# RWKV-7 half of a two-layer trunk: TensorE's projections and a recurrence round's ScalarE work put into written-out orders

## The chip, the cores and the metric

The kernel runs on one core of a Trainium2 chip. The metric is the device time of one execution in microseconds (us); lower is better. Each version's time is the median of several runs.

## The reference, cut to what matters

The reference is one inference step of a two-layer trunk on 1104 tokens: a prompt of 1024 tokens behind 16 learned meta tokens, and 8 sampled sequences of 8 tokens each. Layer 0 is a gated DeltaNet layer, which the change does not touch. Layer 1 is RWKV-7 time mixing, of which this much matters here:

```python
xs = xn[None] + xx[None] * mu[:, None, None, :]            # six mixes with the token before
rkvz = jnp.einsum('sbtd,sde->sbte', xs[:4], w_rkvz)        # r, k, v, z: four 1024 x 1024 projections
...
def step(S, inp):
    r_t, k_t, v_t, d_t, kk_t, b_t = inp
    S = (S * d_t[:, :, None, :]
         + jnp.einsum('bhvk,bhk->bhv', S, -kk_t)[..., None] * b_t[:, :, None, :]
         + v_t[..., None] * k_t[:, :, None, :])
    return S, jnp.einsum('bhvk,bhk->bhv', S, r_t)
...
y = (y - mean) * lax.rsqrt(var + GN_EPS) * lnx_w.reshape(H, N) + lnx_b.reshape(H, N)   # per head
y = y + jnp.sum(r_h * k_h * r_k, -1, keepdims=True) * v_h                              # bonus
y = y.reshape(B, T, D) * jax.nn.silu(z)
return y @ w_o, S, xn[:, -1]
```

There are 16 heads of 64. The data is float32.

## The kernel before, in words

**Numbers.** A product of two float32 matrices is made as three matmuls: each factor is split into a high part (a copy by ScalarE, line 86, such as `whi` of a weight tile `wraw`) and the rest (a subtraction on GpSimd, or sometimes VectorE, line 90, such as `wlo`), and high x high, high x low and low x high are summed. A weight tile has 8 blocks of 128 rows, so a projection tile of 128 outputs by up to 384 tokens is 24 matmuls. Tokens come in three segments: 384, 384 and 336.

**The stages of layer 1**, by the time at which they stand in the profile:

- about 1360 to 1475: the decay and rate terms and the key projection (`keys_decay_rate`).
- about 1475 to 1860: the projections r, v and z (`project`; z only for two segments, the third is left to the recurrence). Each starts with `mix`: for 8 blocks of 128 channels and each segment, ScalarE scales the tokens, VectorE adds the scaled tokens before them (tile `mixs`, line 1071), ScalarE takes the high part and VectorE or GpSimd the low one (tiles `xa`, `xc`, `xh`, `xl`). The tiles of a projection's input are reused by the next one. Beside the projections the *systems* are set up (`rwkv_inverse`): the tokens are cut into chunks of 64, six chunks of one pair of heads and one segment are an *item*, and there are 8 pairs x 3 segments = 24 items in five batches. For each item VectorE, ScalarE and GpSimd prepare `skk` and `sal`, TensorE makes 24 small matmuls `fL` (shown as x12 pairs in an order) and two `frss`, and VectorE copies the latter out (`rkc`). For each batch VectorE then inverts blocks by substitution (`invtmp`, `invT`, lines 444 and 446), and a *merge* for each item joins two 32 x 32 inverses into a 64 x 64 one: matmuls `mY`, a VectorE scaling `invY`, matmuls `mU` (`inverse_merge`).
- about 1860 to 2421: the recurrence (`wave`). It runs in rounds, tau = -3 to 53; an item takes six rounds, one for each chunk, a new item starts every second round, and so up to three items of different pairs are in a round. A round is a chain: *solve and scores* on TensorE from the state (`rA<-rS,AR`), `X` on ScalarE (line 62), the *inner* matmuls (`rA<-X,rTT`), `UV` on ScalarE, then the new state and the outputs from `UV` (`rA<-UV,BT` and `rA<-UV,G`), the state update `rS` on VectorE (line 1470), which needs `pre`, the decayed old state, from ScalarE, and the outputs `y` (line 1481). One PSUM tile `rA` of each item holds all of these products. The next round's solve needs `rS`.

**What fills a round.** Between the steps of the chain stand pieces of other work: the preparation of the next item (`rwkv_front`: loads `fldk`, `flda` and others, ScalarE's `fkk`, `fDp`, `fiD`, `k`, `prh`, GpSimd's and VectorE's products, TensorE's `fG`, `fBT`, `fVT`, `fbonus`, and the copies `BT` and `UV` out of PSUM), GroupNorm and the gate of finished items (`rwkv_finish`, whose product `lz` is split into `yh` and `yl` for the output projection), and *jobs* handed out by `fill` at steps that a table of start and end rounds sets: first the gates of the third segment (matmuls `zz`, six to a step), then output projections (`zo` and `do`), each of which starts by splitting two weight tiles on ScalarE and GpSimd.

**What sets the order.** A scheduler simulates the program's time line and puts each engine's instructions in order from that; `high_priority` moves an instruction ahead in its choice. In a block under `manual_schedule` for TensorE, TensorE's instructions stay in the order in which the code emits them. Before the change, the recurrence is under it (so TensorE's order there is the code's, and the other engines' is the scheduler's), and the projections are not: there the scheduler orders all engines. Every engine works through its own list in order and waits at an instruction whose inputs are not ready.

## Time and profile before

| | us |
|---|---|
| median of 3 runs (lowest 2412.68, highest 2417.64) | 2412.91 |
| the profiled execution | 2422.7 |
| its span | 2421.0 |
| granted TensorE clock over the span | 0.967 of full speed |
| TensorE busy | 2213.4 |
| VectorE busy | 1620.5 |
| ScalarE busy | 1279.8 |
| GpSimd busy | 1049.8 |

The profile names TensorE's matmuls PE and its weight loads PEld, VectorE DVE, ScalarE ACT and GpSimd POOL. A row names the engine, the line of the code, the operation and the tiles: `PE L80 rA<-UV,G` is a matmul on line 80 into `rA` from `UV` and `G`. Most matmuls of the recurrence and of the projections are recorded on lines 76 and 80, which are helpers, so they are told apart by their tiles. In a list of waits, "A <- B: 24.0, 47, 2.2" says that A waited for B 24.0 us in all, 47 times, 2.2 us at most. In a time line a bracket at a row's end says how long the engine was idle before that row and for what. Durations of matmuls include their way through the array, so that successive ones overlap.

### The profile page before, as it was taken

To read this page: it belongs to the slowest core of one execution; us is meant where nothing else is said; L and a number is where in the kernel's file an instruction comes from. 1 tells how busy PE (TensorE), PEld (TensorE's weight loads), DVE (VectorE), ACT (ScalarE), POOL (GpSimd) and SP (SyncE) were. 2 spreads that over 40 slices of the span, in tenths; PEclk is the share of its full clock that TensorE was granted. 3 is DMA by queue.
4 is the path that set the end of the run, shared out by engine and by line. 5 is a ranking of instruction groups with operands and counts; after the bars stand their busy time and mean duration, and the time that the engine had idled before them with its cause. 6 is when DMAs were issued, how large, how long until landed. Compare 5 with 4: busy or idle time off the path is not lost. (4 is left out here: it accounts for less than half of the span.)

```text
span 2421.0 us, 54809 instructions
## 1 busy us (share of the span) xinstructions
PE 2213.4 (91%) x19737; PEld 2003.7 (83%) x19737; DVE 1620.5 (67%) x4201; ACT 1279.8 (53%) x3665; POOL 1049.8 (43%) x1446
## 2 busy tenths in 40 slices
PE   6989999999999999999989998988998888888896
PEld 5888989888898989888989898877787676777775
DVE  6868676776868596863347616588894567667654
ACT  5445555555646565565334647474453555666552
POOL 3435343334434353433314424453354555666643
PEclk9999999999999999999999999999998999999998
DMA  3323333323232333353351344666645435555543
GB/s 110 104 74 101 86 109 86 91 76 99 82 108 61 100 96 89 94 160 114 108 137 61 97 172 153 169 160 172 167 122 173 124 107 149 158 163 156 157 131 117
DMA packets 470924, 290.05 MB, mean 120 GB/s; under 512 B 188506, under 2 KB 456027, under 8 KB 470651
## 3 DMA queue, kind: packets, MB, share of 16 engines
q1 hardware_dynamic: 470650, 286.53, 42.0%
q8 instruction: 156, 2.56, 0.5%
q14 instruction: 118, 0.96, 0.1%
HBM read 200.53 MB, written 85.89 MB: 118 GB/s over the span
## 5 line engine op out<-in xcount | busy, mean ns | idle before, releaser
L90 POOL TENSOR_TENSOR wlo<-wraw,whi 128x512 fp32r<-128x512 f32 (+2 forms) x252 | 331.8, 1319 | 379.9 <-ACT whi L86 361.6
L76 PE MATMUL d<-xc,whi 128*128 128x384 f32 (+2 forms) x910 | 258.3, 341 | 4.5 <-POOL xc L90 2.5
L86 ACT CAST whi<-wraw 128x512 fp32r<-128x512 f32 (+2 forms) x252 | 152.0, 605 | 145.4 <-PE dq L76 50.7
L411 DVE SCALAR_TENSOR_TENSOR cvy<-raw,cw,cvy 128x408 f32<-128x408 f32 (+2 forms) x288 | 179.0, 634 | 16.3 <-ACT cvy L62 14.5
L76 PEld LDWEIGHTS d<-xc,whi 128*128 128x128 f32 (+1 forms) x910 | 167.5, 191 | 10.7 <-issue 3.4
L444 DVE TENSOR_TENSOR invtmp<-invA,invT 72x31 f32<-72x31 f32 (+31 forms) x403 | 165.2, 410 | 14.1 <-DMA invA<-ltd 5.3
L446 DVE TENSOR_TENSOR invT<-invT,invtmp 72x31 f32<-72x31 f32 (+31 forms) x403 | 165.7, 411 | 6.6
L76 PE MATMUL dz<-xc,whi 128*128 128x384 f32 (+1 forms) x480 | 148.9, 341 | 0.0
L76 PE MATMUL dv<-xc,whi 128*128 128x384 f32 (+1 forms) x480 | 146.8, 335 | 0.0
L76 PE MATMUL d<-xc,wlo 128*128 128x384 f32 (+2 forms) x428 | 142.3, 341 | 1.4 <-POOL wlo L90 1.4
L76 PE MATMUL d<-xa,whi 128*128 128x384 f32 (+3 forms) x450 | 139.8, 345 | 3.5 <-DVE xa L90 1.7
L860 POOL TENSOR_SCALAR Sb<-Sb,eglb 128x128 f32<-128x128 f32 x128 | 80.1, 643 | 90.4 <-DMA Sb<-in_state_gdn 46.8
L76 PE MATMUL dv<-xa,whi 128*128 128x384 f32 (+1 forms) x288 | 100.0, 347 | 0.1
L76 PE MATMUL dz<-xa,whi 128*128 128x384 f32 (+1 forms) x288 | 100.1, 348 | 0.0
L76 PEld LDWEIGHTS d<-xa,whi 128*128 128x128 f32 (+1 forms) x450 | 83.1, 190 | 11.5 <-issue 4.5
L76 PEld LDWEIGHTS dz<-xc,whi 128*128 128x128 f32 x480 | 89.4, 192 | 0.8
L76 PEld LDWEIGHTS dv<-xc,whi 128*128 128x128 f32 x480 | 88.6, 188 | 0.5 <-issue 0.4
L80 PE MATMUL rA<-UV,G 128*64 128x64 f32 x1152 | 63.6, 240 | 26.0 <-DVE rS L1470 24.0
L76 PE MATMUL d<-xa,wlo 128*128 128x384 f32 (+3 forms) x252 | 85.5, 339 | 0.0
L62 ACT ACTIVATE o<-rA,gcol 128x128 f32<-128x128 f32 x128 | 46.6, 372 | 73.6 <-DVE S L771 73.3
L76 PE MATMUL d<-xh,wlo 128*128 128x384 f32 (+1 forms) x256 | 84.1, 344 | 1.5 <-POOL wlo L90 1.5
L76 PE MATMUL d<-xh,whi 128*128 128x384 f32 (+1 forms) x256 | 84.2, 344 | 0.7 <-ACT whi L86 0.4
(509 smaller groups left out, 7194.7 us busy)
## 6 DMA issues: line engine op xcount, KB each, us to landing
wraw<-in_gdn_w_in SPq DMA_DIRECT2D x96, 256.0 KB
wraw<-in_rwkv_w_rkvz SPq DMA_DIRECT2D x80, 256.0 KB
Sb<-in_state_gdn SPq DMA_DIRECT2D x64, 256.0 KB
wraw<-in_rwkv_w_o SPq DMA_DIRECT2D x40, 256.0 KB
E<-drow SPq DMA_DIRECT2D x24, 384.0 KB
attn<-drow SPq DMA_DIRECT2D x24, 384.0 KB
wraw<-in_gdn_w_out SPq DMA_DIRECT2D x36, 256.0 KB
out_s_gdn<-Sb SPq DMA_DIRECT2D x32, 256.0 KB
```

Of the source, the lines that this page charges most:

```text
L62: return self.nc.scalar.activation(out, in_, func, bias=bias, scale=scale, **kw)
L76: self.nc.tensor.matmul(out, lhsT, rhs, start=start, stop=stop)
L80: self.nc.tensor.matmul(out, lhsT, rhs, start=start, stop=True, skip_group_check=True)
L86: nc.scalar.copy(hi, x)
L90: e.tensor_tensor(lo, x, hi.bitcast(F32), op=ALU.subtract)
L411: nc.vector.scalar_tensor_tensor(y[:, 0:wd], raw[:, k:k + wd], cw[k], y[:, 0:wd], op0=ALU.mult, op1=ALU.add)
L444: nc.vector.tensor_tensor(tmp, A[:, j, j + 1:32].unsqueeze(2).broadcast_to([nb, n, m]), Tv[:, j, 0:m].unsqueeze(1).broadcast_to([nb, n, m] ...
L446: nc.vector.tensor_tensor(Tv[:, j + 1:32, 0:m], Tv[:, j + 1:32, 0:m], tmp, op=ALU.subtract)
L860: nc.gpsimd.tensor_scalar(Sb[:, u], Sb[:, u], self.eglb[:, hv, 4 * g + u:4 * g + u + 1], None, op0=ALU.mult)
```

## The change

It has two parts.

**Projections.** A new method `projections` runs r, v and z with TensorE in emission order. A projection tile is now emitted segment by segment, 24 matmuls each, and after every 12 there is a *gap* (r 48, v 48, z 32 of them). In each gap one step of the systems is emitted: an item is three empty steps and then its `fL` and `frss` in one, a batch ends with four empty steps and its inversion. A batch's merges stand from the 28th gap after that on, one a gap, `mY` in one and `mU` in the next. The last tile of k is emitted in the same manner, without systems. Two stretches of TensorE's order where r gives way to v (`d` are the projection's matmuls, `fL` an item's, `mY` a merge's, `fbpp` a transposition for a batch's scales). Before, with the last rows of r's tile `d_20109` and the first of `d_20809`:

```order
L76 MATMUL d_20109<-xh_2813_15540,wlo_20050 128x336
L76 MATMUL mY_18871<-T1n_18730,L_3313_18731 32x32
L76 MATMUL d_20109<-xl_2814_15541,whi_20049 128x336
L76 MATMUL d_20109<-xh_2815_15542,whi_20049 128x336
L76 MATMUL d_20109<-xh_2815_15542,wlo_20050 128x336
L76 MATMUL mY_18871<-T1n_18730,L_3313_18731 32x32 x11
L73 MATMUL fbpp_19534<-ident_74,invR_19532 128x30
L76 MATMUL d_20109<-xl_2816_15543,whi_20049 128x336
L76 MATMUL fL_20159<-sal_20154,skk_20139 64x64 x12
L76 MATMUL d_20809<-xc_114,whi_20799 128x384
```

After, with the last row of r's tile `d_19895` and the first of v's tile `d_20128`:

```order
L76 MATMUL d_19895<-xl_2816_15543,whi_19794 128x336
L76 MATMUL mY_19920<-T1n_18865,L_3332_18866 32x32 x12
L76 MATMUL fL_19936<-sal_19875,skk_19860 64x64 x12
L76 MATMUL frss_19937<-sgl_19873,hmask_84 2x384
L76 MATMUL d_20128<-xc_114,whi_20118 128x384
L76 MATMUL d_20128<-xc_114,wlo_20119 128x384
L76 MATMUL d_20128<-xc_114,whi_20118 128x384 x2
L76 MATMUL d_20128<-xc_114,wlo_20119 128x384
L76 MATMUL d_20128<-xc_114,whi_20118 128x384
```

Before, single matmuls of a merge stand between single matmuls of a tile, and a tile may begin before another ends; now a tile's segment runs through, and a merge's `mY`, an item's `fL` and its `frss` stand whole in the gap between two.

**Recurrence.** The state and the outputs of an item are emitted together, and then its `rS` and `y`. TensorE's order at the end of a round of three items, before (state products from `BT` for all items, then output products from `G`):

```order
L80 MATMUL rA_29327<-UV_4127_23281,BT_28194 64x64 x2
L80 MATMUL rA_29333<-UV_4128_23282,BT_28504 64x64 x2
L80 MATMUL rA_29340<-UV_4129_23283,BT_28858 64x64 x2
L80 MATMUL rA_29327<-UV_4127_23281,G_28193 64x64 x2
L80 MATMUL rA_29333<-UV_4128_23282,G_28503 64x64 x2
L80 MATMUL rA_29340<-UV_4129_23283,G_28857 64x64 x2
```

After:

```order
L80 MATMUL rA_29249<-UV_4126_23283,BT_27951 64x64 x2
L80 MATMUL rA_29249<-UV_4126_23283,G_27950 64x64 x2
L80 MATMUL rA_29255<-UV_4127_23284,BT_28249 64x64 x2
L80 MATMUL rA_29255<-UV_4127_23284,G_28248 64x64 x2
L80 MATMUL rA_29261<-UV_4128_23285,BT_28563 64x64 x2
L80 MATMUL rA_29261<-UV_4128_23285,G_28562 64x64 x2
```

A round's output products now follow each item's state products at once.

`pre` moves from the end of the solve to behind the inner matmuls (`step_old`), and all of ScalarE's work that the code emits behind the inner matmuls of a round (`issue_after`) is tied behind the last `UV` of that round. The pieces stand in another order: `front` for the next item is emitted at the end of an even round, the gates begin two rounds earlier with an extra step of `fill` in the rounds before tau = 0, `rwkv_finish` has one step more, and a new output projection's weight splits come with the `fill` behind the inner matmuls. ScalarE's order where the second kind of job, an output projection, begins, before (`whi` is the first of its two weight tiles, `X` and `UV` belong to the second round before the one in which its matmuls `zo` start):

```order
L86 CAST whi_28101<-wraw_28099 128x512
L1396 COPY BT_27312<-fBT_27707 128x384
L62 ACTIVATE X_27759<-rA_27758,rk_10_97 128x64
L62 ACTIVATE X_27765<-rA_27764,rk_10_97 128x64
L86 CAST yh_27754<-lz_27418 128x384
L62 ACTIVATE k_5144_27885<-flda_27866,omka_23270,pcol_384 128x384
L62 ACTIVATE X_27772<-rA_27771,rk_10_97 128x64
L62 ACTIVATE UV_4126_23280<-rA_27758 64x128
L62 ACTIVATE UV_4127_23281<-rA_27764 64x128
L62 ACTIVATE UV_4128_23282<-rA_27771 64x128
L62 ACTIVATE fiD_28169<-fldcs_28156 128x384
L86 CAST prh_27894<-pr_27892 128x384
```

After, the rows behind the three `UV` of the round whose matmuls `zo` follow its inner matmuls and read these `whi`:

```order
L62 ACTIVATE pre_28144<-rS_4123_23280,DC_27036 128x64
L62 ACTIVATE pre_28146<-rS_4124_23281,DC_27334 128x64
L62 ACTIVATE pre_28148<-rS_4125_23282,DC_27632 128x64
L86 CAST yh_28150<-lz_27759 128x384
L86 CAST whi_28156<-wraw_28154 128x512
L86 CAST whi_28164<-wraw_28162 128x512
L62 ACTIVATE fkk_28221<-fldk_28213,pcol_384 128x384
L62 ACTIVATE fDp_28223<-fldcs_28211 128x384
L62 ACTIVATE fiD_28224<-fldcs_28211 128x384
L62 ACTIVATE k_5209_28234<-flda_28215,omka_23273,pcol_384 128x384
L86 CAST prh_28243<-pr_28241 128x384
L1501 COPY y_27519<-rA_28097 128x64
```

Before, this split stands two rounds ahead of its use and in front of a round's `X`, and `X`, `yh`, `k` and `X` alternate; now the splits stand behind `UV`, `pre` and `yh`, and `y`, the copies of the round's outputs, stand behind the next item's `fkk`, `fDp`, `fiD`, `k` and `prh`.

Third, GroupNorm's normalisation, two GpSimd operations on 128 x 384 with broadcast operands (lines 1500 and 1501), becomes six operations on 128 x 64 with a scalar for each partition.

```diff
...
+        yield
         pU = self.ps("m", 2, "U")
...
-    def project(self, m, k, x, dst, apart=False):
+    def project(self, m, k, x, dst, gap=None):
         nc, t = self.nc, self.t
-        w = self.load_w(self.i["rwkv_w_rkvz"][0, m][:, 128 * k:128 * k + 128])
-        ps = (self.dense(w, 128, *x, s, bufs=4) for s in range(2 if m == 3 else 3)) if apart else self.dense3(w, 128, *x)
-        for (c0, n), p in zip(SEGS, ps):
+        his, los = w = self.load_w(self.i["rwkv_w_rkvz"][0, m][:, 128 * k:128 * k + 128])
+        ps = zip(SEGS, self.dense3(w, 128, *x)) if gap is None else ((c, self.ps("d", 4)) for c in SEGS[0:2 if m == 3 else 3])
+        for (c0, n), p in ps:
+            if gap is not None:
+                c = 0
+                for q in range(8):
+                    wh, wl = his[q // 4][:, q % 4], los[q // 4][:, q % 4]
+                    a, b = x[0][q][:, c0:c0 + n], x[1][q][:, c0:c0 + n]
+                    for l, r in ((wh, a), (wl, a), (wh, b)):
+                        self.mm(p[:, 0:n], l, r, start=c == 0, stop=c == 23)
+                        c += 1
+                    if q % 4 == 3:
+                        gap()
...
             nc.vector.tensor_tensor(kk, kk, iD, op=ALU.mult)
+            for _ in range(3):
+                yield
             gp = self.ps("f", 2, "L")
...
+        for _ in range(4):
+            yield
         rk2 = self.rk2[:, 30 * b:30 * b + nth]
         blk = self.block_scale(ssd, rk2, pool)
         TT = [t(pool, [128, 6, 64], "sTT", 3) for _ in items]
         T1n, L21 = t(pool, [128, 30, 32], "T1n", 1), t(pool, [128, 30, 32], "L21", 1)
         self.inverse_blocks(f"r{b}", ltd, blk, pool, TT, T1n[:, 0:nth], L21[:, 0:nth], nth)
-        for q, n in enumerate(items):
-            self.inverse_merge(L21, TT[q], T1n, rk2[:, 6 * q:6 * q + 6], pool, 6 * q, 6)
-            nc.sync.dma_start(self.ttd[n], TT[q].rearrange("p c k -> p (c k)"))
+        def merge(q):
+            m = self.inverse_merge(L21, TT[q], T1n, rk2[:, 6 * q:6 * q + 6], pool, 6 * q, 6)
+            next(m)
+            yield
+            next(m, None)
+            nc.sync.dma_start(self.ttd[items[q]], TT[q].rearrange("p c k -> p (c k)"))
+        merges.extend(merge(q) for q in range(len(items)))
...
+    def step_old(self, P, ci):
+        if 6 * P.s + ci > 1:
+            P.pre = self.t(self.ap, [128, 64], "pre", 3)
+            self.act(P.pre, self.S[P.p], AF.Identity, scale=P.DC[:, ci:ci + 1])
...
+        pA, G, BT, UV, S, DC = P.pA, P.G, P.BT, P.UV, self.S[P.p], P.DC
         hs = [slice(0, 64), slice(64, 128)]
+        if c > 0:
+            for h in (0, 1):
+                self.mmx(pA[hs[h], 384:448], BT[:, ci, hs[h]], UV[:, ci, h, :])
         for h in (0, 1):
+            self.mmx(pA[hs[h], 256:320], G[:, ci, h, 64:128], UV[:, ci, h, :])
+        if c > 0:
+            with self.tc.high_priority():
+                if c == 1:
+                    nc.vector.tensor_scalar(S, pA[:, 384:448], DC[:, ci:ci + 1], None, op0=ALU.mult)
+                else:
+                    nc.vector.scalar_tensor_tensor(S, pA[:, 384:448], DC[:, ci:ci + 1], P.pre, op0=ALU.mult, op1=ALU.add)
...
-        b6 = lambda x: x.unsqueeze(2).broadcast_to([128, 6, 64])
-        nc.gpsimd.tensor_tensor(y6, y6, b6(mv[:, :, 0]), op=ALU.subtract)
-        nc.gpsimd.tensor_tensor(y6, y6, b6(rs), op=ALU.mult)
+        for q in range(6):
+            nc.gpsimd.tensor_scalar(y6[:, q], y6[:, q], mv[:, q, 0:1], rs[:, q:q + 1], op0=ALU.subtract, op1=ALU.mult)
...
         nc.vector.scalar_tensor_tensor(zg[:, 0:n], t1[:, 0:n], self.lnb[:, p:p + 1], zg[:, 0:n], op0=ALU.add, op1=ALU.mult)
+        yield
         yh, yl = t(self.fin, [128, 384], "yh", 7, F32R), t(self.fin, [128, 384], "yl", 7, F32R)
         self.split(zg[:, 0:n], yh[:, 0:n], yl[:, 0:n])
...
+    def projections(self, xa, xb, ip):
+        slots = {0: (0, 1, 2, 3, 4, 5, 9, 10), 2: (6, 7, 8, 0, 1, 2, 9, 10), 3: range(3, 11)}
+        now, wait, under, merges = [0], [], [], []
+        def systems():
+            for b in range(5):
+                yield from self.rwkv_inverse(b, ip, merges)
+                wait.extend((now[0] + 28 + n, m) for n, m in enumerate(merges))
+                merges.clear()
+        sy = systems()
+        def gap():
+            now[0] += 1
+            for m in under:
+                next(m, None)
+            under.clear()
+            while wait and wait[0][0] <= now[0]:
+                m = wait.pop(0)[1]
+                next(m)
+                under.append(m)
+            next(sy, None)
+        for m in (0, 2, 3):
+            x = self.mix(m, xb, slots[m], SEGS[0:2] if m == 3 else SEGS)
+            for k in range(8):
+                self.project(m, k, x, {0: self.rd, 2: self.vd, 3: self.zd}[m], gap)
+                if (m, k) == (3, 0):
+                    zin = self.gate_inputs(xa, xb)
+        while wait or under:
+            gap()
+        return zin
...
-        jobs = [(gates, 33, -2.5, 14), (lambda: out(0, 0, 4, Z), 17, 14, 22), (lambda: out(0, 4, 8, DD), 17, 22, 30),
+        jobs = [(gates, 33, -4.5, 14), (lambda: out(0, 0, 4, Z), 17, 14, 22), (lambda: out(0, 4, 8, DD), 17, 22, 30),
...
+        def front(tau):
+            if tau % 2 and (tau + 3) // 2 < 24:
                 s, p = divmod((tau + 3) // 2, 8)
                 P[8 * s + p] = self.rwkv_front(p, s)
+        front(-3)
+        for tau in range(-3, 55):
             m = (tau + 2) // 2
             parts = P[m].parts[3 * (tau % 2):3 * (tau % 2) + 3] if 0 <= m < 24 else [[], [], []]
             items = [(P[n], tau - 2 * n) for n in range(max(0, (tau - 4) // 2), min(24, tau // 2 + 1)) if 0 <= tau - 2 * n < 6]
+            each = lambda *fs: [f(*x) for f in fs for x in items]
+            ins = each(self.step_solve, self.step_scores)
+            if tau < 0:
+                fill(tau + 0.3)
+            for f in parts[0]:
+                f()
+            ins = each(self.step_inner)
+            with self.tc.issue_after(ins[-1]) if ins else ExitStack():
+                each(self.step_old)
+                if tau % 2 == 0 and 0 <= (tau - 8) // 2 < 24:
+                    next(P[(tau - 8) // 2].done, None)
+                fill(tau + 0.5)
+                for f in parts[1]:
+                    f()
+                for Q, ci in items:
+                    if ci == 1 and Q.s == 0:
+                        late.append(self.rwkv_sample_write(Q.p, Q, Q.BT, Q.UV, Q.DC))
+                late = [x for x in late if not next(x, True)]
+                each(self.step_state)
+                fill(tau + 1)
+                for f in parts[2]:
                     f()
                 late = [x for x in late if not next(x, True)]
+                for Q, ci in items:
+                    if ci == 5:
+                        Q.done = self.rwkv_finish(Q.p, Q.s, Q)
+                        next(Q.done)
+                if tau % 2 and 0 <= (tau - 7) // 2 < 24:
+                    next(P[(tau - 7) // 2].done)
+                front(tau + 1)
         fill(99)
```

More of the change, by code (lines that the diff above doesn't have):

```diff
@@ L1748, in layer1 @@
         self.rwkv_masks(ip, True)
[L1749 to L1758 removed]
+        with tc.manual_schedule(engines={mybir.EngineType.PE}):
+            zin = self.projections(xa, xb, ip)
         ctx.close()
@@ L1845, in wave @@
                     f()
                 late = [x for x in late if not next(x, True)]
-                if g == 0:
-                    for Q, ci in items:
-                        if ci == 1 and Q.s == 0:
-                            late.append(self.rwkv_sample_write(Q.p, Q, Q.BT, Q.UV, Q.DC))
-                            next(late[-1])
-            for Q, ci in items:
-                if ci == 5:
-                    Q.done = self.rwkv_finish(Q.p, Q.s, Q)
-                    next(Q.done)
-            if (tau - 7) % 2 == 0 and 0 <= (tau - 7) // 2 < 24:
-                next(P[(tau - 7) // 2].done, None)
```

47 lines of the change are left out of this document (3 added, 44 removed).

## The prediction, made before the changed kernel was run

> **What bounds the kernel now.** I read the page first, then the busy times by stage, then what TensorE (PE) waits for in each stage, and last the time line of two rounds.
>
> ```profile
> span 2421.0 us, 54809 instructions
> PE 2213.4 (91%) x19737; PEld 2003.7 (83%) x19737; DVE 1620.5 (67%) x4201; ACT 1279.8 (53%) x3665; POOL 1049.8 (43%) x1446
> PE 17%; DVE 6%; DMA 3%; issue 2%; ACT 1%; POOL 1%; SPq 0%; DVEq 0%; POOLq 0%; ACTq 0%
> ```
>
> TensorE is busy for 91% of the span and leads the chain, so what can be won without taking matmuls away is its idle time and its slow clock. The change touches the time from 1475 us on. By stage (us, busy time and count of PE, PEld, DVE, ACT, POOL; then granted clock, DMA share, GB/s):
>
> ```profile
> 1475.00:1860.00 385.00, 350.99 (x3297) 309.15 (x3295) 278.38 (x589) 198.09 (x427) 169.54 (x255) 0.95 0.61 159
> 1860.00:1900.00 40.00, 30.03 (x254) 25.65 (x254) 23.91 (x44) 16.36 (x36) 24.45 (x35) 0.83 0.55 164
> 1900.00:2380.00 480.00, 420.90 (x5587) 358.46 (x5583) 321.23 (x903) 268.58 (x853) 271.00 (x306) 0.97 0.49 145
> 2380.00:2421.00 41.00, 23.25 (x139) 20.09 (x139) 17.08 (x43) 10.18 (x28) 14.01 (x20) 0.83 0.22 70
> ```
>
> In the projections TensorE idles 385 - 351 = 34 us and loses about 5% of 385 = 19 us to the clock: 53 us. In the recurrence it idles 10 us at the start, 59 us in the steady part and 18 us at the end; the clock takes 3% of 480 = 14 us and 17% of 40 = 7 us. The waits of TensorE in the recurrence (total us, times, longest):
>
> ```profile
> PE rA L80 <- DVE rS L1470: 24.0, 47, 2.2
> PE rA L80 <- ACT X L62: 20.1, 19, 1.9
> PE rA L80 <- DVE X L1440: 5.8, 5, 4.0
> ...
> PE rA L80 <- ACT y L1481: 3.9, 6, 1.5
> ```
>
> **The rS wait goes: -24 us.** At the end of a round stand:
>
> ```profile
> 2145.59 0.78 ACT L62 ACTIVATE UV<-rA 64x128 f32<-64x128 f32 x3
> ...
> 2147.60 0.57 PE L80 MATMUL rA<-UV,BT 128*64 128x64 f32 x12
> 2148.18 0.66 DVE L1470 SCALAR_TENSOR_TENSOR rS<-rA,DC,pre 128x64 f32<-128x64 f32 x3
> ...
> 2148.51 0.72 PE L80 MATMUL rA<-UV,G 128*64 128x64 f32 x12 [0.34 <-DVE rS L1470]
> ...
> 2150.74 0.68 PE L80 MATMUL rA<-rS,AR 64*64 64x64 f32 x15
> ```
>
> The output products into `rA` start only when VectorE has read the state out of the same `rA`, 47 times for 0.5 us. With each item's output products emitted right behind its state products, nothing that VectorE reads lies between them; `rS` follows both, and 2.2 us of filler (2148.51 to 2150.74) still hide it from the next solve. I take the whole row; the bound below is half of it, if `rS`, now later by an item's products, meets the solve.
>
> **The X wait goes: -18 of 20.1 us.** In every second round ScalarE (ACT) is caught by other work while TensorE needs `X`:
>
> ```profile
> 2162.34 0.51 ACT L86 CAST yh<-lz 128x384 fp32r<-128x384 f32 x1 [1.32 <-DVE lz L1509]
> 2162.76 0.70 ACT L62 ACTIVATE k<-flda,omka,pcol 128x384 f32<-128x384 f32 x1
> 2163.37 0.29 ACT L62 ACTIVATE X<-rA,rk 128x64 f32<-128x64 f32 x1
> 2163.69 0.78 ACT L62 ACTIVATE UV<-rA 64x128 f32<-64x128 f32 x3
> 2163.72 0.45 PE L80 MATMUL rA<-X,rTT 128*64 128x64 f32 x4 [1.55 <-ACT X L62]
> ```
>
> `yh`, which itself waited 1.32 us for VectorE, and `k` stand ahead of the third `X`. In the new order they stand behind `UV`, and the three `X` and three `UV` follow one another. I leave 2 us for rounds in which a `y` or a copy of the round before is late.
>
> **The clock behind short waits: -8 us in the recurrence.** The 4 us behind the wait just shown:
>
> ```profile
> 2164.00:2168.00 4.00, 3.96 (x33) 3.27 (x33) 3.07 (x8) 1.44 (x4) 1.92 (x2) 0.58 0.91 275
> ```
>
> A wait of 1.55 us was followed by a granted clock of 0.58: some 1.7 us lost. With most of the X waits gone I take back 8 of the 14 + 7 us; the rest stays with the other waits. The Trainium skill, page "TensorE: Matmul & The Clock Gate", section "Why this matters for your kernels", says that the clock falls only after TensorE was idle for a whole window, above about 3 us. This row disagrees: 1.55 us were enough. By the page these 8 us, and 7 more below, would not come.
>
> **The start: -4 us.** The first rounds have nothing between solve and inner (the DVE X row, 5.8 us). The change puts 24 `zz` matmuls there, each about 0.18 us at the rate quoted below: 4 us of work done inside waits.
>
> **New waits on ScalarE: +17.5 and +6 us.** Durations on ScalarE and GpSimd (count, busy us, mean ns, idle before):
>
> ```profile
> L62 ACT ACTIVATE pre<-rS,DC 128x64 f32<-128x64 f32 x127 | 39.7, 343 | 19.8 <-DVE rS L1470 19.0 <-DVE rS L1468 0.2
> L86 ACT CAST whi<-wraw 128x512 fp32r<-128x512 f32 x49 | 30.4, 621 | 23.1 <-PE zo L76 9.8 <-PE zz L76 5.8 <-PE do L76 5.7
> L62 ACT ACTIVATE fkk<-fldk,pcol 128x384 f32<-128x384 f32 x20 | 12.3, 616 | 20.9 <-DMA fldk<-kd 20.3 <-POOL BK L1356 0.4
> L62 ACT ACTIVATE fiD<-fldcs 128x384 f32<-128x384 f32 x20 | 10.4, 522 | 18.5 <-DVE BK L1355 18.5
> ...
> L90 POOL TENSOR_TENSOR wlo<-wraw,whi 128x512 fp32r<-128x512 f32 x54 | 71.2, 1319 | 49.7 <-ACT whi L86 49.7
> ...
> L1500 POOL TENSOR_TENSOR y<-y,mv 128x384 f32<-128x384 f32 x24 | 20.0, 833 | 39.8 <-ACT y L1481 24.0 <-DVE mv L1495 13.5 <-DVE bnst L1494 2.0
> ...
> L1342 POOL COPY DC<-fDp 128x6 f32<-128x6 f32 x22 | 6.3, 284 | 23.0 <-DVE rS L1470 22.1 <-ACT fDp L62 0.9
> ```
>
> First, an output projection's first weight tile is now split in the round whose `zo` or `do` needs it, right behind the inner matmuls, where it stood two rounds earlier before. From the inner's end: `UV` 0.8 us, three `pre` 3 x 0.34 = 1.0, `yh` 0.5, `whi` 0.6, then `wlo` on GpSimd 1.3: 4.2 us until the first matmul that reads `wlo`. The filler that stands there, six such matmuls and two of the bonus (8 x 0.18 = 1.4 us), covers in other rounds the `UV` copies; here most of it comes after the wait. 4.2 + about 0.7 of it still to run - 1.4 = 3.5 us a switch, five switches (rounds 14, 22, 30, 38, 46): 17.5 us. Bounds: 0, if an earlier `whi` of the running job leaves the round short enough, to 21 (4.2 each).
>
> Second, `y` now stands behind `pre`, `yh`, `whi`, `fkk`, `fDp`, `fiD` and `k` in even rounds: 1.0 + 0.5 + 0.6 + 0.6 + 0.5 + 0.5 + 0.7 = 4.4 us behind `UV`, and a solve writes the `rA` that `y` reads (the row PE rA <- ACT y shows that wait). In the first time line `UV` ended at 2145.59 + 0.78 = 2146.37, and the solve began at 2150.74, 4.4 us later. The margin is nothing; I put 0.3 us on 20 such rounds, 6 us, from 0 to 25 (rival 2).
>
> **GroupNorm: +1 us.** Two operations of 0.83 us become six of 128x64; each lies between 0.28 us (the 128x6 copy) and 0.83, and I take 0.45, nearer the small one: 2.7 us against 1.7 for an item. GpSimd is busy 271 of 480 us in the steady part and hides it; at the end, where nothing else runs, it costs 1 us.
>
> Recurrence: -24 - 18 - 8 - 4 + 17.5 + 6 + 1 = **-29.5 us**.
>
> **Projections: -14 us.** TensorE waits there:
>
> ```profile
> PE fL L76 <- DVE skk L1299: 11.0, 5, 3.4
> PE mY L76 <- DMA T1n<-r_t: 4.7, 3, 4.1
> ```
>
> The new order gives an item three gaps and a merge 28 before TensorE needs them, so these go. What comes in their place is that TensorE can't pass a matmul whose tile of the mix is late. Pieces of the chain, and VectorE where r gives way to v:
>
> ```profile
> 1803.12 17.39 PE d L76 x98
> ...
> 1724.81 0.84 PE fL L76 x24
> 1725.65 0.74 PE frss L76 x2
> ...
> 1749.93 0.50 PE mU L76 x24
> ```
>
> ```profile
> 1586.35 0.54 DVE L1313 COPY rkc<-frss 2x384 f32<-2x384 f32 x1
> ...
> 1625.57 0.49 DVE L90 TENSOR_TENSOR xl<-mixs,xh 128x336 fp32r<-128x336 f32 x1
> ...
> 1636.28 1.37 DVE L446 TENSOR_TENSOR invT<-invT,invtmp 120x231 f32<-120x231 f32 x1
> ```
>
> ```profile
> 1600.00:1650.00 50.00, 44.58 (x504) 37.05 (x504) 47.78 (x95) 36.35 (x85) 27.01 (x35) 0.92 0.62 169
> ```
>
> VectorE is busy 47.78 of 50 us there with 95 instructions, 0.50 us each. In the new order 83 of them stand between the `rkc` of batch 2's first item and the last low part of v's mix: 83 x 0.50 = 42 us (before, 1586.35 to 1626.06: 40 us from the last item of batch 1). TensorE has from that item's `frss` to v's first tile's need of this part 4 segments of 24 at 17.39 / 98 = 0.177 us, two shorter ones at 336/384 of that, three items of 0.84 + 0.74 = 1.6 and five merges of 1.0 us (`mY` and `mU`, 0.50 each): 17.0 + 7.4 + 4.7 + 5.0 - 0.6 = 33.5 us. So it stalls 42 - 33.5 = 8 us. From k to r, where the mix runs likewise just ahead, I put the same 8; from v to z nothing, since only 14 instructions (7 us) stand there against 18 us of matmuls. Merges and items that find VectorE late: 11 us, as much as the `skk` row. The clock keeps 12 of its 19 us. 8 + 8 + 11 + 12 = 39 against 53 now: **-14 us**. Bounds: -33 (only the transition's 8 and the clock stay) to +40 (rival 3).
>
> **The sum.** -29.5 - 14 = -43.5 us on the profiled 2422.7, so 2379; the same on the median 2412.9 gives **2369 us**. A difference of 0.2%, 4.8 us, is about what a measurement of this kernel tells from none.
>
> **The rivals.**
>
> 1. *More is hidden.* The switches cost nothing and neither r-to-v nor late merges and items stall: -43.5 - 17.5 - 8 - 11 = -80, **2333 us**. For it: VectorE is busy only 278 of 385 us over the stage. Against: 47.78 of 50 in the stretch that counts.
> 2. *The copies of y hold the next solve.* In some 20 even rounds `y` also waits behind `fkk` for its load (20.3 us of waiting for `fldk` in the row above, 1 us a time). 1.2 us more in 20 rounds: +24, **2393 us**.
> 3. *Slower: TensorE in order meets VectorE late.* 24 merges follow `mY` with `mU` one gap of 12 x 0.177 = 2.1 us later, and 24 items need `skk` at a set place; VectorE in between may stand in a substitution step of 1.4 us (the row at 1636.28). If each of the 48 meetings costs 1.1 us, 53 instead of 11, and the clock 12 us more, this is +54 on the sum: -43.5 + 54 = +10, **2423 us**. It decides from about 0.9 us a meeting. For it: before, 5 such waits of up to 3.4 us in spite of free order. Against: VectorE's idle share outside the transitions.
> 4. *Nothing measurable*, as when filler is only used up earlier and the rounds grow elsewhere: **2413 us**.
> 5. *The half clock does not hang on the short waits* and stays: 8 + 7 us do not come, -28.5, **2384 us**. Against: the 0.58 behind 1.55 us. This is also what the page named above would give.
>
> **How the numbers follow.** Forecast 0.45 (own range 2341 to 2395: the switches and the late meetings at nothing, -28, one way; `y` at 1 us a round, +14, and half of the rS row, +12, the other), rival 1 0.13, rival 2 0.17, rival 3 0.14, rival 4 0.07, rival 5 0.04. The range 2332 to 2414 leaves out half of rival 1 and rival 3. Faster: 0.45 + 0.13 + 0.17 + 0.04 = 0.79; same 0.07; slower 0.14.
>
> **What would show it.** In the changed profile: the row PE rA <- DVE rS gone and PE rA <- ACT X near 2 us; at five switches waits of `zo` or `do` for `whi` and `wlo`, some 3.5 us each; a row PE rA <- ACT y of 5 to 8 us; `d` waiting for `xc` or `xl` twice for about 8 us; the projections' stage 371 us instead of 385, the recurrence 531 instead of 561. I am wrong in mechanism if the rS or X waits stay, if merges wait for `invY` by over 50 us, or if the rounds keep their length with TensorE waiting elsewhere.

## The result: slower by 0.9%

| | before | after |
|---|---|---|
| median of 5 runs, us | 2412.91 (2407.43 to 2425.62) | 2433.37 (2423.21 to 2437.51) |
| ratio, 95% interval | 1 | 1.009 [1.0063, 1.0118] |
| profiled execution, us | 2422.7 | 2423.2 |
| its span, us | 2421.0 | 2421.5 |
| granted clock over the span | 0.967 | 0.962 |

Forecast was 2369 us, range 2332 to 2414. The change costs some 20 us. The two profiled executions hide that: the one of before lies 10 us above its median, the one of after is the fastest of its five runs. Much of this arose before the changed part: the same matmul near the start of layer 1 stands 11.1 us earlier in the profile of after (before first, then after):

```profile
1376.48 0.51 PE L76 MATMUL flora<-xa,lw2l 128*128 128x384 f32 x2
```

```profile
1365.38 0.51 PE L76 MATMUL flora<-xa,lw2l 128*128 128x384 f32 x2
```

So stages are compared in the profiles, counted from this matmul on, and the size of an effect on the whole time is taken from the ratios.

TensorE is busy for 91% of the span, as before. The stages are cut at the first `fG` of the recurrence, and the window of after begins 11.1 us earlier. Windows of before, then of after (length, busy time and count of PE, PEld, DVE, ACT, POOL, then clock, DMA share, GB/s):

```profile
1475.00:1860.50 385.50, 350.99 (x3297) 309.15 (x3295) 278.88 (x589) 198.25 (x427) 170.04 (x256) 0.95 0.61 159
1860.50:2421.00 560.50, 474.18 (x5976) 404.19 (x5976) 361.73 (x988) 294.95 (x915) 308.96 (x358) 0.95 0.48 141
```

```profile
1463.90:1875.10 411.20, 357.72 (x3330) 317.63 (x3329) 282.26 (x592) 199.20 (x428) 177.23 (x256) 0.93 0.57 149
1875.10:2421.50 546.40, 463.88 (x5952) 393.46 (x5952) 337.30 (x988) 296.82 (x917) 347.72 (x453) 0.92 0.49 145
```

The projections grew by 25.7 us (TensorE idles 53.5 us in place of 34.5, at a clock of 0.93 in place of 0.95), the recurrence shrank by 14.1 us, and its clock fell from 0.95 to 0.92. Forecast was -14 and -29.5. The growth is well clear of the scatter between profiles: from the matmul above to the first `fG`, the six kernels with the projections of before (before, e1, e6, e7, e8, e10) take 480 to 484 us, the three with the change's (after, e2, e4) 507 to 510. The 14.1 us are less certain: the recurrence of before took 560.5 us here, but 554.0 and 551.5 us in e2 and e9, which have the same code for it. What TensorE waits for in the projections of after (total us, times, longest):

```profile
PE fbpp L73 <- DMA invR<-rssd: 22.0, 4, 7.9
PE fL L76 <- DVE skk L1312: 6.4, 4, 2.8
PE mU L76 <- DVE invY L510: 4.7, 3, 4.0
...
PE mU L76 <- ACT siD L62: 3.1, 2, 2.3
...
PE d L76 <- POOL xa L90: 1.3, 1, 1.3
```

And in the recurrence of after:

```profile
PE zz L76 <- DVE zst L1030: 10.5, 3, 7.8
PE fG L76 <- DVE k L1527: 6.7, 5, 2.6
PE do L76 <- ACT whi L86: 6.6, 6, 2.1
PE zo L76 <- POOL wlo L90: 6.3, 4, 2.0
PE zo L76 <- ACT whi L86: 6.2, 3, 2.1
PE rA L80 <- ACT X L62: 5.1, 8, 2.1
PE do L76 <- POOL wlo L90: 4.7, 4, 1.9
PE rA L80 <- ACT y L1501: 3.3, 11, 0.4
```

The `rS` row (24.0 us) is gone and the X row fell from 20.1 to 5.1 us, as forecast. In their place stand the splits of an output projection (`whi` and `wlo`, 6.6 + 6.3 + 6.2 + 4.7 = 23.8 us, most of it where a new one starts) and the gates' `zz` (10.5). In the projections a row of 22.0 us is new, which no step of the forecast had: `fbpp`, the transposition of a batch's scales, waiting for their load.

### The profile page after: what moved, and what is told of

Its sections match the earlier page's. It is cut to its first block, busy times and chain, and to the rows that moved or that the text cites. A ratio compares the mean times of both kernels' runs of the same rounds, so it can differ in the third digit from the quotient of the medians.

```text
span 2421.5 us, 54718 instructions
## 1 busy us (share of the span) xinstructions
PE 2201.7 (91%) x19737; PEld 1994.8 (82%) x19737; DVE 1601.0 (66%) x4201; ACT 1282.4 (53%) x3665; POOL 1095.6 (45%) x1542
## 4 chain that ended last, share of the span: by engine, by line
PE 51%; DVE 18%; ACT 8%; DMA 8%; POOL 5%; issue 4%; SPq 3%; DVEq 0%; POOLq 0%; ACTq 0%
PE d L76 14%; PE dz L76 7%; DVE invT L446 4%; PE rA L76 4%; DVE invtmp L444 4%; PE dk L76 3%; PE dq L76 3%; PE rA L80 3%; DMA attn<-drow 2%; PE do L76 1%; POOL attn L572 1%; PE rY L76 1%; PE fG L76 1%; DVE cvy L411 1%; PE zo L76 1%
## 5 line engine op out<-in xcount | busy, mean ns | idle before, releaser
L76 PE MATMUL d<-xc,whi 128*128 128x384 f32 (+2 forms) x910 | 264.1, 345 | 2.7 <-ACT ev L1167 1.9
L1520 POOL TENSOR_SCALAR y<-y,mv,grs 128x64 f32<-128x64 f32 x144 | 83.6, 597 | 35.8 <-DVE grs L106 32.8
L76 PEld LDWEIGHTS d<-xc,wlo 128*128 128x128 f32 (+1 forms) x428 | 82.1, 194 | 4.3 <-POOL wlo L90 3.9
```

What stands on the lines that cost most here:

```text
L76: self.nc.tensor.matmul(out, lhsT, rhs, start=start, stop=stop)
L1520: nc.gpsimd.tensor_scalar(y6[:, q], y6[:, q], mv[:, q, 0:1], rs[:, q:q + 1], op0=ALU.subtract, op1=ALU.mult)
```

## The experiments

Ratios are to the kernel before on the same chip. 0.001 is 2.4 us.

| | median, us | ratio, 95% interval |
|---|---|---|
| e1 recurrence part alone | 2396.66 | 0.9945 [0.9925, 0.9964] |
| e2 projections part alone | 2433.36 | 1.0088 [1.0070, 1.0106] |
| e3 change, scales later | 2419.01 | 1.0030 [1.0017, 1.0044] |
| e4 change, splits earlier | 2407.85 | 0.9987 [0.9973, 1.0000] |
| e5 e3 and e4 together | 2392.23 | 0.9914 [0.9899, 0.9928] |
| e6 e7, gates as before | 2370.45 | 0.9823 [0.9806, 0.9840] |
| e7 e1, splits earlier | 2379.37 | 0.9858 [0.9840, 0.9876] |
| e8 state then outputs alone | 2389.57 | 0.9904 [0.9884, 0.9925] |
| e9 new projections, free order | 2423.86 | 1.0050 [1.0035, 1.0066] |
| e10 e6, GroupNorm as before | 2366.47 | 0.9801 [0.9780, 0.9822] |
| e11 e5, gates as before | 2396.91 | 0.9931 [0.9906, 0.9955] |
| e12 e5, last merges earlier | 2385.70 | 0.9919 [0.9894, 0.9944] |
| e13 change, scales sooner in the queue | 2411.73 | 1.0011 [0.9996, 1.0026] |

### Which part costs: e1 and e2

e1 is the kernel before with the change's recurrence, e2 with its projections:

```diff
 e1, against the change
-        with tc.manual_schedule(engines={mybir.EngineType.PE}):
-            zin = self.projections(xa, xb, ip)
+        for n, (m, k) in enumerate(todo):
+            ...
```

> The kernel before with the change's recurrence, GroupNorm and gate part alone; the projections as before. In the two profiles the recurrence (first fG to the end) fell from 560.5 to 546.4 us. Theory A (each part does to the time what its own stage shows): about 14 us faster than before, 2399 us. Theory B (the stage's gain is eaten by a lower clock in most executions, since the changed kernel's other runs lie 10 us above the profiled one): 2410 us or more, no faster than before.

> The kernel before with the change's projections alone; the recurrence as before. In the two profiles the start of the recurrence moved from 1860.5 to 1875.1 us. Theory A: about 15 us slower than before, 2428 us, with waits of fbpp for the DMA of the scales of some 22 us in all and the recurrence back at 560 us. Theory B: 2433 us or more, as slow as the whole change.

The recurrence's part makes the kernel faster by 0.0055 (13 us, about as its stage in the profile), the projections' part slower by 0.0088 (21 us). Theory A holds for e1. In e2 the time is that of theory B, though not by its cause: over its runs the granted clock is 0.968, as against 0.969 before. The 15 us of theory A were read from profiles that differ by 11 us ahead of layer 1; counted from the same matmul, the start of the recurrence moves by 26 us in e2's profile as in that of after. The two ratios add up to 1.0033, below the 1.009 of the whole; that is more than the intervals leave to chance. With the splits repaired it shows again: there the projections cost 31 us (e4 against e7) and not 21. How the parts hinder each other stays open.

### What TensorE stands for in the projections: e3, e13, e9, e12

e3 emits the scales, their transposition and the inversion six gaps later, beside the next batch; the merges keep their gaps:

```diff
         for _ in range(4):
             yield
+        for _ in range(6):
+            yield "ahead"
         rk2 = self.rk2[:, 30 * b:30 * b + nth]
...
-                wait.extend((now[0] + 28 + n, m) for n, m in enumerate(merges))
+                    wait.extend((now[0] + 22 + n, m) for n, m in enumerate(merges))
```

> The change with a batch's scales, their transposition fbpp on TensorE and the inversion behind it emitted six gaps (12 us) later beside the next batch; the merges keep their gaps. Theory A (in the fixed order TensorE stands for the load of the scales, 22.0 us in four waits): the fbpp waits go, the time falls by about 22 us to 2411 us. Rival C (the DMA wait only uncovers another: the inversion, now emitted later, delays the merges, and mU waits for invY or ACT instead): under 8 us gained, 2425 us or more, with mU and mY waits of 15 us or more.

The `fbpp` waits go and 0.006 (14 us) comes back, two thirds of the wait. Theory A has the mechanism. In part another wait comes in its place, as C said, but not the one that C named: `frss` now waits 8.6 us for the reading of the transposed scales. Why is the load late at all? The last `rkc` of the third batch, SyncE's queue and the `fbpp` behind it, time line of after:

```profile
1703.70 0.55 DVE L1328 COPY rkc<-frss 2x384 f32<-2x384 f32 x1
...
1710.94 5.81 SPq L478 DMA_DIRECT2D sTT<-r_u  x12
1716.85 0.25 SPq L1329 DMA_DIRECT2D rssd<-rkc  x1
...
1718.11 0.41 SPq L487 DMA_DIRECT2D invR<-rssd  x1
...
1719.86 0.28 PE L73 MATMUL fbpp<-ident,invR 30*128 30x30 f32 x1 [7.89 <-DMA invR<-rssd]
```

`rkc` is ready at 1704.25, but its store is issued at 1716.85, 12.6 us later, behind other issues, twelve of `sTT` among them that took 5.81 us. Store and load themselves then need 3 us. e13 leaves TensorE's order alone and moves forward only these issues and VectorE's four small operations on the scales:

```diff
-            nc.sync.dma_start(ssd[6 * q:6 * q + 6].rearrange(...), kc.rearrange(...))
+            with self.tc.high_priority():
+                nc.sync.dma_start(ssd[6 * q:6 * q + 6].rearrange(...), kc.rearrange(...))
...
-        blk = self.block_scale(ssd, rk2, pool)
+        with self.tc.high_priority():
+            blk = self.block_scale(ssd, rk2, pool)
```

> The change with the scales' stores and loads given high priority, so that they stand sooner in SyncE's queue; fbpp keeps its place on TensorE. In the changed kernel the last store of the third fbpp's batch was issued 12.6 us behind its rkc, behind 12 issues of sTT that took 5.8 us. In this order the store stands ahead of those twelve, but the load of invR still behind nine issues of them. Theory O (the fbpp wait is SyncE's queue, not the transfer): the waits of fbpp fall from 22.0 us to 12 or less, and the time to 2424 us or less, ratio 1.005. Rival P (the transfers themselves take the time, or another wait follows): fbpp still waits 18 us or more, 1.007 or more.

The waits of TensorE in e13's projections, and the store that came 12.6 us late before:

```profile
PE fL L76 <- DVE skk L1312: 10.3, 5, 4.1
...
PE fbpp L73 <- DMA invR<-rssd: 4.3, 2, 3.0
```

```profile
1701.01 0.55 DVE L1328 COPY rkc<-frss 2x384 f32<-2x384 f32 x1
...
1704.46 0.91 SPq L1330 DMA_DIRECT2D rssd<-rkc  x1
```

The store now goes out 2.9 us behind `rkc`, the waits fall from 22.0 to 4.3 us, and the time from 1.009 to 1.0011: 19 us. Theory O is shown: TensorE stood for SyncE's queue, not for the transfer. What is left of the loss in e13's profile is 15 us from the matmul named above to the first `fG` (499.4 us against 484.0 before).

e9 asks whether the fixed order is needed for the loss at all: the change's projections on the recurrence of before, without the manual schedule.

```diff
-        with tc.manual_schedule(engines={mybir.EngineType.PE}):
-            zin = self.projections(xa, xb, ip)
+        zin = self.projections(xa, xb, ip)
```

> The projections of the change on the recurrence of before, but without the manual schedule: the same instructions in the same emission order, and the scheduler orders TensorE again. The projections in fixed order alone stood at 1.0088 (2433 us). Theory A (the cost is TensorE standing in its fixed order for DMA, VectorE and ScalarE): back to within 5 us of the kernel before, 2417 us or less, with no fbpp wait over 1 us. Rival I (the cost lies in what the new method emits: tiles segment by segment, merges 28 gaps later): 2425 us or more.

1.005 lies between the two theories, and neither's number came: half of e2's loss goes with the fixed order (`fbpp` waits 3.1 us in place of 22.0), half stays. Where the half that stays may lie is seen at the end of the stage. Time line of before (the last merge, a last matmul of z, and the first `fG`), then of e9:

```profile
1846.04 0.57 PE L76 MATMUL mU<-sTT,invY 32*32 32x32 f32 x24
...
1857.00 0.34 PE L76 MATMUL d<-xl,whi 128*128 128x384 f32 x1
...
1860.53 1.42 PE L76 MATMUL fG<-AR,BK 64*128 64x128 f32 x12 [3.19 <-POOL BK L1356]
```

```profile
1854.91 0.57 PE L76 MATMUL mU<-sTT,invY 32*32 32x32 f32 x24
1869.55 1.66 PE L76 MATMUL fG<-AR,BK 64*128 64x128 f32 x12 [14.07 <-POOL BK L1378]
```

The recurrence's first `fG` follows the last `mU` by 14 us in both. Before, the last z tiles run in that time; with merges 28 gaps behind their batch the last one is also the last matmul of the stage, and TensorE idles 14.07 us in place of 3.19. These 11 us are about what stays (0.005, 12 us). No run moves the merges alone in the free order, so this cause is argued and not shown. e12 tries it in the fixed order, on e5, with the last batch's merges six gaps earlier:

```diff
-                    wait.extend((now[0] + 22 + n, m) for n, m in enumerate(merges))
+                    wait.extend((now[0] + (22 if len(merges) == 5 else 16) + n, m) for n, m in enumerate(merges))
```

> The change with the scales later and the first splits earlier (0.9914), and the last batch's four merges six gaps earlier. In each kernel so far the first fG stands 13.3 to 16 us behind the last mU, since the recurrence's loads come only then; with the scales later the last inversion ended at 1826 us and the last mU at 1857. Theory M (the set place of the last merges holds the start of the recurrence): the last mU comes some 12 us earlier, the first fG follows the last z matmul within 3 us in place of 6.6, and 3 to 6 us go: ratio 0.989 to 0.990. Rival N (the merges wait at the new place for their inverse, or the loads were not what held the start): the first fG stays, 0.9914 or more.

In e12's time line the last merge stands 12 us earlier than in e5 (7 us, counted from the first `flora<-xa,lw2l`, at 1374.5 us in e5 and 1369.9 in e12), but the start does not come earlier by that count:

```profile
1845.08 0.57 PE L76 MATMUL mU<-sTT,invY 32*32 32x32 f32 x24
...
1864.50 0.34 PE L76 MATMUL d<-xl,whi 128*128 128x384 f32 x1
...
1869.22 0.94 PE L76 MATMUL fG<-AR,BK 64*128 64x128 f32 x12
```

The ratio is that of e5 (0.9919 against 0.9914): theory N, though the interval does not exclude the 3 us of theory M. The waits of e12's projections show the reason that N gave:

```profile
PE mU L76 <- DVE invY L510: 5.6, 2, 3.0
PE mY L76 <- DMA T1n<-r_t: 4.4, 1, 4.4
```

In e5 `mU` waited 0.9 us for `invY` and `mY` not at all for `T1n`. The merges now reach their place before their inverse is ready, and counted as above the last z matmul comes 5 us later than in e5. The first `fG` no longer waits for `BK` (4.3 us in e5), so what is won there is lost ahead of it. What still separates e5 from e7 is 0.9914 against 0.9858, 13 us. In e5's projections TensorE has many small waits, of `fL`, `frss`, `mU`, and of `d` for `whi`, `wlo` and `xh`. They weren't taken apart, so that they are the cause isn't shown.

### The first splits of an output projection: e4, e5, e7

e4 loads and splits the first weight tile of five output projections one round earlier, still behind that round's `UV`:

```diff
                 each(self.step_old)
+                load_ahead(tau)
...
-        w = load(0)
+        w = w or load(0)
```

> The change with the first weight tile of the five output projections that start in rounds 14, 22, 30, 38 and 46 loaded and split one round earlier, still behind that round's UV. Theory A (zo and do wait for their own split: 23.8 us by whi and wlo in the changed kernel's profile, and rounds with a start are 13.2 to 16 us long against 9.2): some 18 us faster than the change, 2415 us. Rival D (the earlier split holds the earlier round's y and the next X instead): under 5 us, 2428 us or more.

One such start in the time line of after:

```profile
2110.95 0.74 ACT L62 ACTIVATE UV<-rA 64x128 f32<-64x128 f32 x3 [0.74 <-PE rA L80]
2111.71 0.82 ACT L62 ACTIVATE pre<-rS,DC 128x64 f32<-128x64 f32 x3
2112.44 0.49 ACT L86 CAST yh<-lz 128x384 fp32r<-128x384 f32 x1
2112.84 1.14 ACT L86 CAST whi<-wraw 128x512 fp32r<-128x512 f32 x2
2113.51 0.44 PE L76 MATMUL do<-yh,whi 128*128 128x384 f32 x1 [2.13 <-ACT whi L86]
...
2114.66 2.51 POOL L90 TENSOR_TENSOR wlo<-wraw,whi 128x512 fp32r<-128x512 f32 x2
...
2115.99 0.69 PE L76 MATMUL do<-yh,wlo 128*128 128x384 f32 x1 [1.86 <-POOL wlo L90]
```

This is the chain of the forecast, `UV`, `pre`, `yh`, `whi`, `wlo`; TensorE waits 2.13 + 1.86 = 4.0 us, not 3.5, since `yl` stands ahead of `wlo` on GpSimd, and ahead of `yl` GroupNorm's six operations, which keep GpSimd until 2113.7 us. The four us behind it ran at half clock:

```profile
2116.00:2120.00 4.00, 4.00 (x31) 3.45 (x32) 3.96 (x4) 0.00 (x0) 3.03 (x5) 0.50 0.50 151
```

In e4 the rows are down from 23.8 to 4.2 us:

```profile
PE zo L76 <- POOL wlo L90: 2.0, 1, 2.0
...
PE do L76 <- ACT whi L86: 1.2, 3, 0.5
PE do L76 <- POOL wlo L90: 1.0, 2, 0.5
```

0.0103 comes back (25 us), more than theory A's 18, and the recurrence falls from 546.4 to 523.0 us in the profiles. Four of the five starts waited 3.8 to 4.0 us and the first one 2.7, 18.5 us in all; the half clock behind them (0.50 to 0.60 over the next 4 us at each) is the likely rest. e5 has e3's and e4's edits together, e7 e4's edit on e1:

> The change with the scales six gaps later and the five first splits one round earlier. Measured apart these moved it from 1.009 of the kernel before to 1.003 and to 0.9987. Theory A (two separate waits in two stages): the gains add up, ratio 0.9925, about 2393 us. Rival B2 (a shorter projection stage only moves the start of the same recurrence, and the clock takes part of each gain): 0.996 or more, 2402 us.

> The projections as before; the recurrence of the change with the five first splits one round earlier. Theory A: the recurrence alone stood at 0.9945 (2397 us), the earlier splits took another 25 us from the whole change, so 0.984, about 2372 us. Rival D2 (the splits gain less where the rest of the round is less delayed): 0.990 or more, 2387 us.

e5's gains add up (theory A). In e7 the splits win 0.0087 (21 us), near theory A.

### The early gates: e6 and e11

```diff
-            if tau < 0:
-                fill(tau + 0.3)
...
-        jobs = [(gates, 33, -4.5, 14),
+        jobs = [(gates, 33, -2.5, 14),
```

> The projections as before; the recurrence with the five first splits one round earlier, and the gates started in round -2.5 as before, without the extra fill before round 0. The changed kernel's zz waits for zst 10.5 us, 7.8 us of it before round 0. Theory E (zz goes ahead of a buffer that is not free, and TensorE stands there): no slower than the same kernel with the early gates, 2372 us or less. Rival F (24 zz matmuls fill the first rounds, 4 us as predicted): 4 us slower than it, 2376 us or more.

> The change with all three repairs: scales six gaps later, first splits one round earlier, gates as before. Theory A (terms add): 0.9914 less the 0.0035 that the gates gave, 0.988, about 2383 us; against 0.9823 with the projections as before, the fixed order of the projections then still costs some 13 us. Rival L (without the early gates the scales' repair is worth more, since the start of the recurrence was one knot): 0.984 or less, 2374 us.

In e6 the old start of the gates is faster by 0.0035 (8 us, theory E); in e11 it is slower by 0.0017, within its interval, and at 0.9931 both A (0.988) and L (0.984 or less) are missed. So no gain from the early gates is shown, and whether they cost time with the new projections ahead of them is not settled. What they meet is plain in the time line of after:

```profile
1880.44 1.05 DVE L1370 TENSOR_TENSOR AR<-fldr,fDp 128x384 f32<-128x384 f32 x1 [4.95 <-DMA fldr<-rd]
...
1883.74 0.49 DVE L1030 SCALAR_TENSOR_TENSOR zst<-zst,zz 128x336 f32<-128x336 f32 x1
...
1884.29 0.65 PE L76 MATMUL zz<-xa,whi 128*128 128x336 f32 x1 [7.81 <-DVE zst L1030]
```

The gates have one PSUM tile. Its second use must wait until VectorE has read the first (`zst`), and VectorE stands at `AR` for a load. The filler, put there to cover waits, became the wait.

### The rS wait alone, and GroupNorm: e8 and e10

```diff
+            self.mmx(pA[hs[h], 256:320], G[:, ci, h, 64:128], UV[:, ci, h, :])      # in step_state, behind the BT products
...
-            self.mmx(pA[64 * h:64 * h + 64, 256:320], G[:, ci, h, 64:128], UV[:, ci, h, :])   # in step_outputs
```

> The kernel before with one edit: an item's output products are emitted right behind its state products. Theory G (the rS wait, 24.0 us, is lost time of TensorE): the row PE rA from DVE rS goes and the time falls by about 24 us to 2388 us. Rival H (the rounds are held by ScalarE's X and by the fill, and a wait removed turns up in the next one): the row goes, but X and y waits grow by as much, 2405 us or more.

0.9904, 23 us, theory G by its number. The `rS` row is gone; of e8's waits

```profile
PE rA L80 <- ACT X L62: 27.1, 23, 2.5
...
PE rA L80 <- ACT y L1482: 4.4, 6, 1.3
```

X took 7 us more than the 20.1 of before, and `fG` waits 3 us more for the copy `UV`, so part of the wait did turn up in the next ones, as H said. That the sum is still 23 us comes from the end of a round, which shrank by more than the 0.5 us of a wait. In the round at 2147.60 us that the prediction shows, the state and output products took 1.63 us from the first start to the last end; in e8 they take 0.92:

```profile
2099.89 0.34 PE L80 MATMUL rA<-UV,BT 128*64 128x64 f32 x4
...
2100.52 0.29 PE L80 MATMUL rA<-UV,G 128*64 128x64 f32 x4
```

The clock has no part in it: over all runs the mean granted clock is 0.969 in e8 and 0.970 before. e10 puts GroupNorm's two wide operations back into e6:

```diff
-        for q in range(6):
-            nc.gpsimd.tensor_scalar(y6[:, q], y6[:, q], mv[:, q, 0:1], rs[:, q:q + 1], op0=ALU.subtract, op1=ALU.mult)
+        nc.gpsimd.tensor_tensor(y6, y6, b6(mv[:, :, 0]), op=ALU.subtract)
+        nc.gpsimd.tensor_tensor(y6, y6, b6(rs), op=ALU.mult)
```

> The repaired recurrence with the gates as before (0.9823) and GroupNorm's normalisation in two GpSimd operations again. In the changed kernel's profile the six take 6 x 0.597 = 3.6 us an item against 1.7 us. Theory J (GpSimd has room in the rounds; only the last items show it): within 4 us of 0.9823, 2366 to 2372 us. Rival K (GpSimd's splits wlo and yl come late behind the six): 6 us faster or more, 2364 us or less.

0.9801 against 0.9823, 4 us by the medians, with intervals that overlap: nearer theory J than K, and no difference is shown. The operations in the recurrence of after, and in e10:

```profile
L1520 POOL TENSOR_SCALAR y<-y,mv,grs 128x64 f32<-128x64 f32 x144 | 83.6, 597 | 35.8 <-DVE grs L106 32.8 <-PE fG L76 1.6 <-DMA x1T<-zst 1.5
```

```profile
L1499 POOL TENSOR_TENSOR y<-y,grs 128x384 f32<-128x384 f32 x24 | 21.0, 874 | 33.3 <-DVE grs L106 26.0 <-PE rA L80 3.5 <-DVE X L1439 3.2
L1498 POOL TENSOR_TENSOR y<-y,mv 128x384 f32<-128x384 f32 x24 | 20.0, 833 | 21.3 <-DVE mv L1493 13.5 <-DVE bnst L1492 7.7
```

Six operations take 3.6 us an item where two took 1.7. e10 has the lowest time, not to be told from e6: 2366 us, 2% below the kernel before. It has the change's recurrence with the first splits one round earlier, and nothing of the change's projections, early gates or GroupNorm.

## Why the prediction was wrong, step by step

- **The rS wait, -24: right step, and the size in part by luck.** 23 us by e8. But the end of a round shrank by 0.7 us and not only by the wait of 0.5, and some 10 us came back as longer waits for X and `UV`; the prediction had neither, and the two nearly cancel.
- **The X wait, -18: right in kind.** The row fell by 15 us. It was not run alone.
- **The clock, -8: wrong in the change.** The recurrence's clock fell to 0.92 (also in e1). The waits at the five starts and at `zz` put it down where the X waits had before: without the former it is 0.96 (e7), without the latter too 0.98 (e6) and 0.96 (e10), against 0.95 before. Over all runs the mean granted clock is 0.958 in the change, 0.974 in e6 and 0.970 before. So some of the gain came once the new waits were gone, and rival 5 has no support. The reading of the 1.55 us wait was too simple, though. Before, four such waits, at 2089, 2127, 2164 and 2262 us, were followed by clocks of 0.57 or 0.58 over the next 4 us, and four as long, at 2109, 2146, 2183 and 2202, by 1.00; what decides was not tested. Behind the waits of 2.13 and 1.86 us the clock was 0.50. These rows disagree with the 3 us of the Trainium skill's page "TensorE: Matmul & The Clock Gate", section "Why this matters for your kernels": shorter waits were enough here at times.
- **The start, -4: wrong.** The term counted 24 matmuls as cover, and not the one PSUM tile that they share. `zz` waits 10.5 us; what this costs in time is not settled (e6 against e11).
- **The switches, +17.5: right mechanism, too small.** 25 us by e4: up to 4.0 us in place of 3.5, and the half clock behind each.
- **The y copies, +6, and rival 2: wrong.** The row PE rA <- ACT y went from 3.9 to 3.3 us. Rival 2 hung on `fkk` waiting for its load, 20.3 us in the steady part of before; its group in the same part of after (the last number is idle time ahead of it) has none (the next item's loads are now emitted at the end of the round before):

```profile
L62 ACT ACTIVATE fkk<-fldk,pcol 128x384 f32<-128x384 f32 x22 | 13.4, 611 | 0.0
```

- **GroupNorm, +1: not separable**, with 0.60 us an operation in place of the estimated 0.45.
- **Projections, -14: this is the step that failed.** The prediction said that an item gets three gaps and a merge 28 before TensorE needs them, so the waits go. It followed `fL` and `mU`, and left out the third kind of matmul that the generator emits at a set place, `fbpp`, though the order shown ahead of the prediction has it; four gaps (8 us) were what its scales had to get through a store and a load in SyncE's queue. In the scheduler's order of before `fbpp` stood where the load was nearly done (it waited 1.2 us once). In the fixed order it waits 22 us, worth 19 us by e13. The clock's term failed with it: counted as in the prediction, 7% of 411 us, 29 us, went to the clock and not 12. The two transitions, 8 us each, did not come: `d` waits for the mix's tiles 6.7 us in all and 1.5 at most, and in e13, where TensorE hardly stands for `fbpp`, 5.8 and 1.5. The late meetings, 11 us, were about right (6.4 us for `skk`, 7.8 in the two rows of `mU`).
- **Rival 3**, slower, gave 2423 us and came nearest, but by another mechanism: TensorE in a fixed order met SyncE late, not VectorE. Of the 53 us of its late meetings 14 came.

So the recurrence's part won 13 us (e1) where 29.5 were forecast, for the starts cost 25 and not 17.5, the gates met their own buffer and the clock fell; and the projections' part lost 21 us (e2) where 14 were to be won. That e1 and e2 add up to less than the whole change is open, and so are the 13 us that the new projections still cost behind the repair.

## What to carry to other kernels

When an engine is taken out of the scheduler's hands, list every kind of instruction that it now meets at a set place, the small ones too, and follow each back through all the queues that feed it, the queue of DMA issues included: the one left out sets the time. Filler covers a wait only if its own inputs and its own output buffer are ready there. Test the parts of a bundle apart: here one part, repaired, was worth 2%, and the other hid that.

## What the runs showed of the hardware that was not expected

- Twelve DMA issues in a row kept SyncE's queue busy for 5.81 us, 0.48 us each; a store of 3 KB (2x384 float32) that stood behind them and other issues went out 12.6 us late, while store and load together took 3 us.
- GpSimd's 128x64 operation with two scalars took 597 ns, a 128x384 one with broadcast operands 833 ns: a sixth of the elements for 72% of the time (after and e10).
- Of eight waits of TensorE for `X` of about 1.55 us in the profile of before, four were followed by 4 us at a granted clock of 0.57 or 0.58 and four by 4 us at 1.00.
